# Gated attention's level products and value products, issued as two halves of output rows on the two column halves of TensorE

## The chip, the cores and the metric

The kernel runs on one core of one Trainium2 chip. The metric is the device time of one execution in microseconds. The kernel before was run three times: 564.45, 564.78 and 565.18 us, so its median is 564.78 us. Beside these runs stands one execution under the hardware profiler, from which all rows below are taken.

## What is computed

The reference is one layer of a hybrid decoder over 512 tokens of width 1024: an input projection, three groups of attention heads side by side, an output projection, and a feed-forward block of width 4096, with a norm ahead of each and at the end. The change lies in head group B, a gated linear attention with 4 heads of key width 32 and value width 64:

```python
b = jnp.cumsum(chunks(log_a.reshape(Bsz, S, H, dk)), axis=3)
diff = b[..., :, None, :] - b[..., None, :, :]
decay = jnp.exp(jnp.where(causal[:, :, None], diff, NEG_INF))
attn = jnp.einsum('bhnic,bhnjc,bhnijc->bhnij', qc, kc, decay)
o_intra = jnp.einsum('bhnij,bhnjv->bhniv', attn, vc)
...
o_inter = jnp.einsum('bhnic,bhncv->bhniv', qc * jnp.exp(b), s_prev)
o = (o_intra + o_inter).transpose(0, 2, 3, 1, 4).reshape(Bsz, S, H, dv)
```

A query i sees every earlier key j of its chunk, weighted by a decay for each of the 32 key channels; what lies before the chunk comes through a carried state. The inputs are float32.

## The kernel before, in words

**Order of the work.** The kernel is written as generators ("streams": projections, gated attention, softmax attention, weight splitting, loads, feed-forward) that yield operations. Class Plan (L104 to L206) runs them against a small cost model before anything reaches the chip: each operation has a cost (Op, L40 to L82), each engine a clock, and the operation that can start first is issued next, with ties settled by the streams' priorities. What it issues becomes the fixed order of each engine's instructions. So a changed cost can change the order of later instructions, on all engines. A matmul has a mode, which says whether it uses part of the array's rows (32 or 64 of 128) or of its columns; the model adds SWITCH = 0.2 us where the mode changes (L135 to L138). A list of matmuls is issued as one piece.

**Number formats.** The large products run in float32r with operands split in a high and a low part: for each weight, ScalarE copies the high part (tile wh) and VectorE subtracts it to get the low part (tile wl). The gated attention's products are plain float32; in the profile each such matmul shows as two matmul records with two weight loads.

**The gated attention** (gla, L767 to L881) works with chunks of 128 tokens, four of them (NB). Within a chunk the decay is handled by seven levels (LEVELS = 64, 32, ..., 1; L24): at level L, the token pairs in which the query lies in the second half and the key in the first half of the same block of 2L tokens. For each level, VectorE and ScalarE make a tile kq of scaled keys and queries (levels, L883 to L898). Then TensorE multiplies, for each chunk n and head h, the 32 rows of that head: 128 columns of kq as stationary operand, 64 query columns as moving operand, into a PSUM bank lp[h] (L820 to L828). The four heads lie in four row quarters of the array. Levels go in pairs, 32 matmuls at a time, with 16 for the last level alone. The results are copied to the tiles attn[h], by ScalarE for L >= 32 and by VectorE with a mask else (L829 to L843), and the four banks are freed for others.

Beside it, carry (L900 to L947) makes the carried states. Then the output (L848 to L862, PSUM tiles op): for each chunk, one product of eq (decayed queries, 128 x 128) with the masked state smk[n-1] over all 256 value columns, for n of 1 to 3, and four products of attn[h][:, n, :] (128 x 128, stationary) with the 64 value columns of head h. Two VectorE additions (tiles oB) read the result.

**Around it** TensorE does the value projection (v_proj, tiles vps), the query and key projections (qkps) and, for the softmax attention, scores (sps), transposes (ptp) and values (po, L1023 to L1051). VectorE splits weights (wl), adds up the value projection (v), and computes the softmax's P, mn and rz. The values' products po are already placed on the two column halves: each of a pair of heads writes 64 of the 128 output rows.

## Time and profile before

| what | value |
|---|---|
| three runs, median (lowest to highest) | 564.78 us (564.45 to 565.18) |
| the profiled execution's own time | 566.03 us |
| its span, first to last instruction | 564.0 us |
| TensorE busy, share of the span | 553.6 us, 98% |
| TensorE weight loads | 477.8 us, 85% |
| VectorE busy | 479.6 us, 85% |
| ScalarE busy | 370.3 us, 66% |
| mean granted TensorE clock | 0.997 |

In the profile PE is TensorE's matmul, PEld its weight load, DVE is VectorE, ACT is ScalarE, POOL is GpSimd. A row of the timeline gives start, duration, engine, line, operation, the tiles as out<-in, the form, the count, and in brackets the idle time before it with what ended that. Line L133 is the helper that issues every operation, so rows are told apart by tiles. A matmul's form 32*128 32x64 means 32 rows and 128 columns of the array in use and a moving operand of 32 partitions by 64 elements. The ends of matmuls are modelled, so their pace is read from starts. Of the span, 2.03 us of the execution's own time lie outside it.

### The profile page before, as it was taken

To read this page: it belongs to the slowest core of one execution; us is meant where nothing else is said; L and a number is where in the kernel's file an instruction comes from. 1 tells how busy PE (TensorE), PEld (TensorE's weight loads), DVE (VectorE), ACT (ScalarE), POOL (GpSimd) and SP (SyncE) were. 2 spreads that over 40 slices of the span, in tenths; PEclk is the share of its full clock that TensorE was granted. 3 is DMA by queue.
4 is the path that set the end of the run, shared out by engine and by line. 5 is a ranking of instruction groups with operands and counts; after the bars stand their busy time and mean duration, and the time that the engine had idled before them with its cause. 6 is when DMAs were issued, how large, how long until landed. Compare 5 with 4: busy or idle time off the path is not lost.

```text
span 564.0 us, 9463 instructions
## 1 busy us (share of the span) xinstructions
PE 553.6 (98%) x3513; PEld 477.8 (85%) x3513; DVE 479.6 (85%) x874; ACT 370.3 (66%) x659; POOL 69.0 (12%) x90
## 2 busy tenths in 40 slices
PE   8999999999999999999999999999999999999995
PEld 7977887786876768899987899988999888999884
DVE  5799899978867988999799995799957799867985
ACT  5755744694865775989766476855477655579553
POOL 5003110000010002110111010120020110011103
PEclk9999999999999999999999999999999999999998
DMA  8945594685134765992989429687378594395803
GB/s 301 400 121 118 91 261 95 205 320 112 37 43 121 254 146 112 268 274 60 278 212 209 158 64 279 198 149 206 113 162 279 121 201 160 94 216 113 150 18 131
DMA packets 29948, 96.58 MB, mean 171 GB/s; under 512 B 3648, under 2 KB 3690, under 8 KB 29904
## 3 DMA queue, kind: packets, MB, share of 16 engines
q0 software_dynamic: 9456, 33.53, 33.4%
q1 hardware_dynamic: 20160, 62.20, 30.9%
q8 instruction: 27, 0.44, 0.3%
q10 hardware_dynamic: 288, 0.27, 0.1%
q14 instruction: 17, 0.14, 0.1%
HBM read 93.86 MB, written 2.13 MB: 170 GB/s over the span
## 4 chain that ended last, share of the span: by engine, by line
PE 83%; DVE 9%; DMA 3%; ACT 2%; issue 2%; SPq 0%; DVEq 0%; ACTq 0%; POOLq 0%
PE f2X L133 14%; PE f1X L133 13%; PE qkps L133 10%; PE f1Z L133 8%; PE f2Z L133 7%; PE ops L133 7%; PE vps L133 5%; PE f1Y L133 4%; PE f2Y L133 3%; DMA wraw<-in_w 3%; PE ptp L133 3%; PE po L133 2%; DVE wl L133 2%; PE sps L133 2%; PE av L133 1%
## 5 line engine op out<-in xcount | busy, mean ns | idle before, releaser
L133 DVE TENSOR_TENSOR wl<-wraw,wh 128x1024 fp32r<-128x1024 f32 (+2 forms) x174 | 192.0, 1110 | 39.5 <-ACT wh L133 39.1
L133 ACT ACTIVATE wh<-wraw 128x1024 fp32r<-128x1024 f32 (+2 forms) x173 | 164.6, 966 | 58.1 <-DMA wraw<-in_w 12.3
L133 PE MATMUL f1X<-yp,wh 128*128 128x256 f32 x512 | 92.7, 283 | 0.0
L133 PEld LDWEIGHTS f1X<-yp,wh 128*128 128x128 f32 x512 | 80.1, 192 | 0.3
L133 POOL DMA_DIRECT2D wraw<-in_w x46 | 40.5, 948 | 270.2 <-DVE wl L133 227.2
L133 PE MATMUL f1X<-yp,wl 128*128 128x256 f32 x256 | 72.5, 283 | 0.0
L133 PE MATMUL f2X<-wh,Al 128*128 128x512 f32 (+1 forms) x132 | 50.6, 383 | 0.0
L133 PE MATMUL f2X<-wh,Ah 128*128 128x512 f32 (+1 forms) x132 | 50.6, 383 | 0.0
L133 PE MATMUL f2X<-wl,Ah 128*128 128x512 f32 (+1 forms) x132 | 50.5, 383 | 0.0
L133 PEld LDWEIGHTS f1X<-yp,wl 128*128 128x128 f32 x256 | 49.1, 192 | 0.1
L133 PE MATMUL f1Z<-yp,wh 128*128 128x256 f32 x256 | 46.3, 283 | 0.0
L133 ACT ACTIVATE h<-h 128x512 f32<-128x512 f32 x56 | 34.7, 625 | 10.5 <-DVE h L133 9.9
L133 PE MATMUL qkps<-xh,wh 128*128 128x512 f32 x96 | 40.1, 418 | 0.0
L133 PEld LDWEIGHTS f1Z<-yp,wh 128*128 128x128 f32 x256 | 39.9, 192 | 0.0
L133 ACT ACTIVATE P<-P,mn 128x512 f32<-128x512 f32 (+3 forms) x48 | 26.5, 555 | 18.8 <-DVE mn L133 18.8
L133 ACT ACTIVATE Ah<-h 128x512 fp32r<-128x512 f32 x40 | 24.0, 620 | 21.5 <-DVE h L133 21.5
L133 PE MATMUL qkps<-xh,wl 128*128 128x512 f32 x96 | 37.6, 392 | 0.0
L133 PE MATMUL qkps<-xl,wh 128*128 128x512 f32 x96 | 37.5, 390 | 0.0
L133 PE MATMUL f1Z<-yp,wl 128*128 128x256 f32 x128 | 36.2, 283 | 0.0
L133 DVE TENSOR_TENSOR Al<-h,Ah 128x512 fp32r<-128x512 f32 x40 | 26.9, 686 | 3.2 <-ACT Ah L133 3.1
L133 PEld LDWEIGHTS f2X<-wl,Ah 128*128 128x128 f32 x132 | 24.8, 188 | 4.9
L133 PEld LDWEIGHTS f2X<-wh,Ah 128*128 128x128 f32 x132 | 24.8, 188 | 4.8
(264 smaller groups left out, 1220.8 us busy)
## 6 DMA issues: line engine op xcount, KB each, us to landing
wraw<-in_w SPq DMA_DIRECT2D x66, 512.0 KB, 5.2
wraw<-in_w POOLq DMA_DIRECT2D x46, 512.0 KB, 6.7
wraw<-in_wqk SPq DMA_DIRECT2D x12, 512.0 KB, 6.0
wraw<-in_wv SPq DMA_DIRECT2D x10, 512.0 KB, 6.7
wraw<-in_wv POOLq DMA_DIRECT2D x8, 512.0 KB, 5.4
wraw<-in_wo SPq DMA_DIRECT2D x8, 512.0 KB, 7.1
wraw<-in_wo POOLq DMA_DIRECT2D x8, 512.0 KB, 5.5
nb<-tab SPq DMA_DIRECT2D x12, 256.0 KB, 3.5
```

What stands on the lines that cost most here:

```text
L133: getattr(getattr(self.nc, op.eng), op.method)(*op.args, **op.kw)
```

## The change

The level products are issued in two halves: output rows 0 to 63 for all four heads, then rows 64 to 127, each with half of the stationary columns. The value products likewise, the two halves of a head one after the other; the three products with the carried states now all come ahead of them, and they alone carry the flag that starts an accumulation (start=n < 3: chunks 1 and 2, the first into each of the two banks). Two costs of the model are changed. The amount of arithmetic and the copies out of PSUM stay as they are.

```diff
             elif wide and inner[-1].shape[0] == 32:
-                self.cost = 0.031
+                self.cost = 0.0155
             elif wide:
-                self.cost = 0.002 + max(n / 600 / (1 + (args[0].shape[0] == 64)), 0.21)
+                self.cost = 0.002 + max(n / 600, 0.21) / (1 + (args[0].shape[0] == 64))
...
                 for n in range(NB):
-                    for h in range(4):
-                        c = kq[32 * h:32 * h + 32, n * 128:(n + 1) * 128]
-                        o = lp[h][:, i * 256 + n * 64:i * 256 + (n + 1) * 64]
-                        ops.append(PE.matmul(o.rearrange("p (m l) -> p m l", l=L), c,
-                                             c.rearrange("p (m l) -> p m l", l=2 * L)[:, :, L:], start=True, stop=True))
+                    for rows in (slice(0, 64), slice(64, 128)):
+                        for h in range(4):
+                            c = kq[32 * h:32 * h + 32, n * 128:(n + 1) * 128]
+                            o = lp[h][rows, i * 256 + n * 64:i * 256 + (n + 1) * 64]
+                            ops.append(PE.matmul(o.rearrange("p (m l) -> p m l", l=L), c[:, rows],
+                                                 c.rearrange("p (m l) -> p m l", l=2 * L)[:, :, L:], start=True, stop=True))
...
+        for n in range(1, NB):
+            ops.append(PE.matmul(op_[n // 2][:, n % 2 * 256:n % 2 * 256 + 256], eq[:, n * 128:(n + 1) * 128], smk[n - 1],
+                                 start=n < 3, stop=False, skip_group_check=True))
         for n in range(NB):
-            o = op_[n // 2][:, n % 2 * 256:n % 2 * 256 + 256]
-            vb = vB[n // 2][:, n % 2, :]
-            if n:
-                ops.append(PE.matmul(o, eq[:, n * 128:(n + 1) * 128], smk[n - 1], start=True, stop=False, skip_group_check=True))
-            ops.extend(PE.matmul(o[:, h * 64:(h + 1) * 64], attn[h][:, n, :], vb[:, h * 64:(h + 1) * 64],
-                                 start=(n == 0 and h == 0), stop=h == 3, skip_group_check=True) for h in range(4))
+            for h in range(4):
+                for c in (0, 64):
+                    ops.append(PE.matmul(op_[n // 2][c:c + 64, n % 2 * 256 + h * 64:n % 2 * 256 + (h + 1) * 64],
+                                         attn[h][:, n, c:c + 64], vB[n // 2][:, n % 2, h * 64:(h + 1) * 64],
+                                         start=False, stop=h == 3, skip_group_check=True))
```

## The prediction

> **What bounds the kernel now.** I read the page's totals first, then the chain of waits through the stage that the change touches, then busy times by stage.

> ```profile
> PE 553.6 (98%) x3513; PEld 477.8 (85%) x3513; DVE 479.6 (85%) x874; ACT 370.3 (66%) x659; POOL 69.0 (12%) x90
> ```

> TensorE is busy 98% of the span, so it looks as if any time taken from it shortens the kernel. The chain of waits says where that holds:

> ```profile
> 56.94 1.94 PE lp L133 x64
> 58.88 2.95 PE vps L133 x12
> ...
> 64.43 1.94 PE lp L133 x64
> 66.37 10.42 PE vps L133 x45
> 76.80 1.94 PE lp L133 x64
> 78.74 6.81 PE vps L133 x29
> 85.58 0.67 DVE wl L133
> ...
> 94.83 1.13 DVE wl L133
> ...
> 109.61 0.74 PE ptp L133 x4
> ```

> Three of the four groups of level products (tiles lp) are links of the chain. But at 85.58 us the chain goes over to VectorE and comes back to TensorE only at 109.61. The fourth group (last start at 91.5, by a row below) and the output products (op, from 98.45) lie in that stretch, off the chain. The stages in numbers (us, busy and number of records by engine, granted clock, DMA share and rate):

> ```profile
> 57.00:85.00 28.00, 28.00 (x294) 23.60 (x295) 26.07 (x56) 17.34 (x33) 4.35 (x5) 1.00 0.79 180
> 85.00:104.00 19.00, 19.00 (x133) 15.81 (x133) 19.00 (x44) 10.16 (x18) 0.00 (x0) 1.00 0.37 95
> 104.00:110.00 6.00, 5.51 (x32) 3.83 (x29) 6.00 (x25) 3.93 (x13) 0.00 (x0) 1.00 0.69 198
> 125.00:175.00 50.00, 50.00 (x294) 36.36 (x295) 37.82 (x103) 31.75 (x77) 3.50 (x4) 1.00 0.40 85
> ```

> From 85 to 110 us the third busy column, VectorE, is full: 19.00 of 19.00 and 6.00 of 6.00. TensorE is full too up to 104, and from 104 to 110 it has 0.49 us of idle time. Two engines run abreast, and the later one sets the date at which the stage ends. After that TensorE alone is full (50.00 of 50.00, VectorE 37.82) and carries any lead or delay on to the end. That TensorE already waits for VectorE at the end of the stretch is told by two rows of its timeline:

> ```profile
> 106.91 0.83 PE L133 MATMUL sps<-k,q 64*128 64x256 f32 x6 [0.22 <-DVE mn L133]
> 109.61 0.74 PE L133 MATMUL ptp<-cst,P 128*128 128x128 f32 x4 [0.27 <-DVE P L133]
> ```

> Scores wait for a bank that the softmax's first step reads (mn), transposes for its last (P). A TensorE that gets there sooner waits longer.

> **The change, part by part. Level products.** Under the tile lp the trace counts:

> ```profile
> L133 PE MATMUL lp<-kq x224: 267/270/321, 56.9 to 91.5; 32*128 32x64 f32 x112
> ```

> These 224 records become 448. Four heads run side by side on four row quarters, so 224 are 56 rounds. By the chain's row a group of 64 takes 1.94 us, 0.121 a round or 0.030 a record. What fills a round? Weight loads of op and po (ns, shortest, median and longest), and the list op in the timeline:

> ```profile
> L133 PEld LDWEIGHTS op<-vB,attn x32: 187/192/192, 98.2 to 103.1; 128*128 128x128 f32 x32
> ```

> ```profile
> L133 PEld LDWEIGHTS po<-th,v x96: 132/137/137, 125.9 to 208.1; 128*64 128x64 f32 x96
> ```

> ```profile
> 98.45 1.00 PE L133 MATMUL op<-vB,attn 128*128 128x64 f32 x8
> 99.28 0.65 PE L133 MATMUL op<-m,eq 128*128 128x256 f32 x2
> 99.77 1.00 PE L133 MATMUL op<-vB,attn 128*128 128x64 f32 x8
> ...
> 103.35 1.07 PE L133 MATMUL sps<-k,q 64*128 64x384 f32 x12
> ```

> A weight load of 64 columns lasts 137 ns against 192 for 128 columns: 64 columns cost 55 ns, 128 cost 110. Streaming: the two 256-column records take 99.77 - 99.28 = 0.49 us, 245 ns each, so 64 columns take 61 at most. The eight 64-column records of op ahead of them take 99.28 - 98.45 = 0.83, 104 each, which is a weight load and not the stream. So the level products' 121 ns are a load of 128 columns too, and halves would need 61. That two column halves work at the same time is seen in po:

> ```profile
> 198.86 2.30 PE po L133 x16
> ```

> Its 16 records stream 2 x 2 x (512 + 384 + 256 + 128) = 5120 columns; at 0.96 ns a column one after another that is 4.9 us, and it took 2.30. If eight tiles run abreast, 56 rounds save 121 - 61 = 60 ns each, 3.4 us. Rounds of four may hold other costs (op's pace is 104, not 121), so I take 104 - 55 = 49 ns, 2.7 us in all: 0.8 for each whole group, 0.4 for the fourth. Ends: 3.4 us saved, or worse than nothing if starts have a pace of their own (a rival below).

> **Output products.** 32 records at 104 ns become 32 pairs at 61: 3.33 - 1.95 = 1.4 us saved. The move of the three state products (tiles eq) to the front changes nothing in their number; the price is one more change of the array's tiling, from whole to halves, since the scores that follow have a tiling of their own already. Its price stands around the first group of level products:

> ```profile
> 56.55 0.39 PE L133 MATMUL vps<-wl,xh 128*128 128x512 f32 x1
> 56.87 2.01 PE L133 MATMUL lp<-kq 32*128 32x64 f32 x64
> 58.81 0.50 PE L133 MATMUL vps<-wh,xh 128*128 128x512 f32 x1
> 59.15 0.40 PE L133 MATMUL vps<-wh,xl 128*128 128x512 f32 x1
> ```

> From 56.55 to 56.87 pass 0.32 us and from 58.81 to 59.15 0.34, where such records otherwise follow each other by 0.23 (6.81 us for 29 in the chain): 0.1 us each way, 0.2 together. So the output products save 1.2 us, and 1.4 if the change of tiling hides. The third state product now stands ahead of all value products, so it needs its masked state sooner, by the 24 value records at 104 ns that stood before it (2.5 us), and all value products queue behind it on TensorE. That state is made by VectorE; a wait for it falls into time that is free, as follows.

> **What reaches the end.** TensorE has 2.7 + 1.2 = 3.9 us less to do before 106.91, but the scores there wait for VectorE. VectorE's own work is unchanged: the same copies of the same tiles (attn<-lp), the same additions. It can only end sooner by idle time that goes. Between 57 and 85 it has 28.00 - 26.07 = 1.93 us of that, and after 85 none. The gaps, and what ScalarE (ACT) was doing:

> ```profile
> 61.41 0.43 DVE L133 TENSOR_TENSOR kq<-kB,e 128x256 f32<-128x256 f32 x1 [0.38 <-ACT e L133]
> 64.08 0.43 DVE L133 TENSOR_TENSOR kq<-kB,e 128x256 f32<-128x256 f32 x1 [1.23 <-ACT e L133]
> 81.23 1.23 DVE L133 TENSOR_TENSOR wl<-wraw,wh 128x1024 fp32r<-128x1024 f32 x1 [0.29 <-ACT wh L133]
> ```

> ```profile
> 58.96 1.90 ACT L133 ACTIVATE attn<-lp 64x256 f32<-64x256 f32 x7 [0.27 <-PE lp L133]
> 80.13 1.06 ACT L133 ACTIVATE wh<-wraw 128x1024 fp32r<-128x1024 f32 x1 [2.96 <-PE vps L133]
> ```

> ```profile
> 60.00:64.00 4.00, 4.00 (x25) 3.46 (x24) 2.46 (x7) 3.84 (x12) 0.33 (x1) 1.00 0.73 123
> ```

> The first two gaps wait for the exponentials (e) on ScalarE, which between 60 and 64 is itself busy 3.84 of 4.00 us, mostly with copies of lp. It starts those at 58.96 after 0.27 us of waiting for TensorE; with the group done 0.8 us sooner that wait goes, and all that follows moves up by 0.27 at most. The third gap, 0.29, ends on a weight copy that waited 2.96 us for TensorE; by then TensorE is 2.4 us ahead (three groups), so it goes. Together 0.56 us, and with pauses too short for a bracket some 0.6. Bounds: 0, and all 1.93. I take 0.6, the sum of the waits that have TensorE behind them. After 110 us TensorE carries these 0.6 us to the end. One place can eat them, a wait between 264 and 300 us (us in total, times, longest):

> ```profile
> PEld f2Z L133 <- issue: 0.8, 1, 0.8
> ```

> If its cause does not move up, nothing is left; so 0 stays an end. The profiled execution took 566.03 us (span 564.0 and 2.03 around it), 1.25 above the median of the three runs. On its own time the forecast is 565.4, on the median 564.2.

> **The model's costs.** A level group costs the planner the same as before (64 x 0.0155 = 32 x 0.031), so the order up to op should stay. The list op goes from 3 x 0.429 + 16 x 0.212 = 4.68 to 3 x 0.429 + 32 x 0.107 + 0.2 = 4.91, and po's two shortest products in each pair of heads fall from 0.212 to 0.109, 0.21 a pair, 1.2 over six. From op on, other items can thus win a place. The price by rows: a weight split (wl, 1.13 in the chain) that comes ahead of the softmax or behind it, or 0.2 for a pair of tiling changes; either sign.

> **The rivals.** *Slower: starts have a pace of their own.* Now a record starts every 30 ns on average. If that is not four loads in one round but what starts cost, whatever tile they go to, 448 records take 13.6 us instead of 6.8, the output products 64 x 0.03 = 1.9 instead of 3.3, and TensorE is late by 6.8 - 1.4 + 0.2 = 5.6; the 0.49 us of waits vanish, and the time is 564.8 + 5.1 = 569.9. It decides from 15 ns a start upwards, where halves no longer shorten a group. For it: no row shows a closer mean pace. Against it: op's single tile and lp's four have nearly the same round, 104 and 121 ns, which a price for each start does not explain. [...]

> *Halves take turns.* If two halves of one row quarter load one after the other, a round of eight is two of 55 and more, and nothing is gained: 564.8. Against it stands po, though with 128 rows, not 32.

> *The lead is kept.* If VectorE is not what ends the stage, because the new order takes a weight split out of its way, up to 3.9 us arrive: 560.9; with one split of 1.13 out of the way 0.6 + 1.1, 563.1. Against it: 25.00 of 25.00 us of VectorE.

> *A worse order.* Two weight splits ahead of the softmax, 2.3 us, less 0.6: 566.5. One of them, 565.3, is no measurable loss.

> **How the numbers follow.** A measurement of this kernel can tell about 0.2%, 1.1 us, from no change. Forecast (VectorE keeps the date, 0.6 us gained): 0.52, with its own range from 562.85 (all of 1.93) to 564.8; 0.12 of that is beyond 1.1 us. Halves take turns: 0.10. The lead is kept, wholly or in part: 0.14. A worse order: 0.16, 0.09 of it measurable. Starts' own pace: 0.08. So faster 0.12 + 0.14 = 0.26, slower 0.09 + 0.08 = 0.17, same 0.57. The range leaves out the starts' pace and the far end of the kept lead: it goes from 562.0 (two splits out of the way, 0.6 + 2.2) to 566.8 (the worse order and 0.3, about half of the 0.73 between the shown runs).

> **What would show it.** Right: groups lp of 128 records in 1.1 to 1.3 us, op's group done in some 3.7 instead of 4.9, VectorE still full from 85 to 109, and the idle time of TensorE near 107 to 110 grown from 0.5 to nearly 4 us (3.9 less 0.6 more). Wrong: lp groups of 1.9 us or more (no concurrency, or the pace of starts), VectorE with idle time before 109 (then the lead should have been kept), or an order of wl and P that differs there.

## The result, and the profile after

The changed kernel took 571.31 us (median of five runs, 565.28 to 572.10) beside 565.18 for the kernel before (five runs, 564.45 to 565.94). The ratio on record is 1.0074 with an interval of 1.0049 to 1.0099 (that of the two medians alone is 1.011): slower by 0.7 to 1.1%, where 564.2 us and "no measurable change" were forecast. The changed kernel's five runs also lie further apart, 6.8 us against 1.5; a cause has to explain that too. Three runs of later kernels lie over 1.5% above the fastest of their kernel and are left out of the ratios: 572.16 us in experiment 2, and 680.04 and 1611.22 us in experiments 9 and 10, where nothing on record tells the cause.

The profiled execution of the changed kernel took 568.78 us, span 566.8. The totals hardly differ from before:

```profile
PE 553.2 (98%) x3769; PEld 476.7 (84%) x3769; DVE 479.2 (85%) x870; ACT 372.0 (66%) x663; POOL 69.0 (12%) x90
```

The chain of waits through the stage (start, us, engine, tile, count):

```profile
56.31 1.52 PE lp L133 x91
...
63.40 1.52 PE lp L133 x89
64.93 10.43 PE vps L133 x45
75.36 1.66 PE lp L133 x79
77.02 2.97 issue
79.99 0.36 PE lp L133 x7
80.36 9.11 PE vps L133 x39
```

A group of level products now takes 1.52 us instead of 1.94 (the chain's counts leave out some of the 128 records). The third group stops for 2.97 us, and the chain names no releaser: "issue" means that nothing which the profile shows was waited for. TensorE's timeline there, and at the output products:

```profile
75.29 1.73 PE L133 MATMUL lp<-kq 32*64 32x64 f32 x116
79.99 0.36 PE L133 MATMUL lp<-kq 32*64 32x64 f32 x12 [2.97 <-issue]
...
99.27 1.05 PE L133 MATMUL op<-m,eq 128*128 128x256 f32 x4
100.49 0.70 PE L133 MATMUL op<-s2m,eq 128*128 128x256 f32 x2 [0.17 <-DVE s2m L133]
101.12 2.09 PE L133 MATMUL op<-vB,attn 128*64 128x64 f32 x64
103.14 1.08 PE L133 MATMUL sps<-k,q 64*128 64x384 f32 x12
...
108.15 0.82 PE L133 MATMUL sps<-k,q 64*128 64x256 f32 x6 [1.68 <-DVE mn L133]
109.45 0.66 PE L133 MATMUL ptp<-cst,P 128*128 128x128 f32 x2 [0.47 <-DVE P L133]
```

The stop comes after 116 of 128 records of one list, whose products have their operands already. The output products take 103.14 - 99.27 = 3.87 us instead of 4.90. The two waits for VectorE have grown from 0.22 and 0.27 to 1.68 and 0.47.

The same stretches as before, and then two cut at the places where the granted clock changes (us, busy and records of PE, PEld, DVE, ACT, POOL, granted clock, DMA share, GB/s):

```profile
57.00:85.00 28.00, 25.03 (x431) 20.61 (x415) 23.76 (x50) 15.94 (x31) 4.10 (x5) 1.00 0.77 183
85.00:104.00 19.00, 18.83 (x205) 14.81 (x203) 19.00 (x45) 9.49 (x16) 0.25 (x1) 1.00 0.35 85
104.00:110.00 6.00, 3.84 (x22) 2.86 (x21) 6.00 (x20) 3.94 (x11) 0.00 (x0) 0.92 0.74 206
...
105.64:109.05 3.41, 1.65 (x10) 0.96 (x8) 3.41 (x13) 1.60 (x4) 0.00 (x0) 1.00 0.78 175
109.05:112.47 3.42, 3.02 (x8) 2.14 (x8) 2.70 (x13) 2.90 (x12) 0.00 (x0) 0.50 0.95 371
```

VectorE is full from 85 to 110 as before, but up to 85 it idles 28.00 - 23.76 = 4.24 us instead of 1.93: the stop has reached it. And TensorE runs at half clock from 109.05 to 112.47, behind a stretch of the same length in which it was busy for 1.65 of 3.41 us only; that costs up to 3.42 x 0.5 = 1.7 us. The kernel before has no such stretch: its granted clock is 1.00 from 4.44 to 560.81 us.

Where 2.75 us (568.78 - 566.03) came from, by rows of both timelines. The first group starts 0.63 sooner (56.31, and 56.94 by the chain of before), before any edit has acted. The third starts 1.44 sooner (75.36, 76.80), the value projection behind it 1.62 later (80.36, 78.74): a swing of 3.06, the stop. The scores that wait for VectorE start 1.24 later (108.15, 106.91). Far behind the stage a feed-forward product waits for its weight, in the kernel before and after:

```profile
299.73 0.47 PE L133 MATMUL f2Z<-wh,Ah 128*128 128x512 f32 x1 [0.43 <-ACT wh L133]
```

```profile
302.87 0.47 PE L133 MATMUL f2Z<-wh,Ah 128*128 128x512 f32 x1 [0.41 <-ACT wh L133]
```

It is 3.14 late: 1.9 more since the scores, of which the half clock accounts for up to 1.7.

### The profile page after: what moved, and what is told of

Same layout as the page of the kernel before. It is cut to its first block, busy times and chain, and to the rows that moved or that the text cites. A ratio compares the mean times of both kernels' runs of the same rounds, so it can differ in the third digit from the quotient of the medians.

```text
span 566.8 us, 9972 instructions
## 1 busy us (share of the span) xinstructions
PE 553.2 (98%) x3769; PEld 476.7 (84%) x3769; DVE 479.2 (85%) x870; ACT 372.0 (66%) x663; POOL 69.0 (12%) x90
## 4 chain that ended last, share of the span: by engine, by line
PE 86%; DVE 8%; issue 2%; ACT 2%; DMA 2%; ACTq 0%; POOLq 0%; DVEq 0%
PE f2X L133 14%; PE f1X L133 13%; PE qkps L133 10%; PE f1Z L133 8%; PE f2Z L133 7%; PE ops L133 7%; PE vps L133 6%; PE f1Y L133 4%; PE f2Y L133 3%; PE ptp L133 3%; PE po L133 2%; PE sps L133 2%; DVE wl L133 2%; PE av L133 2%; DMA wraw<-in_w 2%
## 5 line engine op out<-in xcount | busy, mean ns | idle before, releaser
L133 DVE TENSOR_TENSOR wl<-wraw,wh 128x1024 fp32r<-128x1024 f32 (+2 forms) x174 | 191.8, 1109 | 38.9 <-ACT wh L133 36.9
L133 ACT ACTIVATE wh<-wraw 128x1024 fp32r<-128x1024 f32 (+2 forms) x173 | 164.3, 966 | 59.0 <-DMA wraw<-in_w 10.0
L133 PE MATMUL f1X<-yp,wh 128*128 128x256 f32 x512 | 92.7, 283 | 0.0
L133 PEld LDWEIGHTS f1X<-yp,wh 128*128 128x128 f32 x512 | 80.1, 192 | 0.3
L133 POOL DMA_DIRECT2D wraw<-in_w x46 | 40.5, 948 | 270.0 <-DVE wl L133 227.1
L133 PE MATMUL f1X<-yp,wl 128*128 128x256 f32 x256 | 72.5, 283 | 0.0
L133 PE MATMUL f2X<-wh,Al 128*128 128x512 f32 (+1 forms) x132 | 50.5, 383 | 0.0
L133 PE MATMUL f2X<-wh,Ah 128*128 128x512 f32 (+1 forms) x132 | 50.5, 383 | 0.0
L133 PE MATMUL f2X<-wl,Ah 128*128 128x512 f32 (+1 forms) x132 | 50.5, 383 | 0.0
L133 PEld LDWEIGHTS f1X<-yp,wl 128*128 128x128 f32 x256 | 49.1, 192 | 0.0
L133 PE MATMUL f1Z<-yp,wh 128*128 128x256 f32 x256 | 46.3, 283 | 0.0
L133 ACT ACTIVATE h<-h 128x512 f32<-128x512 f32 x56 | 34.7, 625 | 10.5 <-DVE h L133 9.9
L133 PE MATMUL qkps<-xh,wh 128*128 128x512 f32 x96 | 40.2, 419 | 0.0
L133 PEld LDWEIGHTS f1Z<-yp,wh 128*128 128x128 f32 x256 | 39.9, 192 | 0.0
L133 ACT ACTIVATE P<-P,mn 128x512 f32<-128x512 f32 (+3 forms) x48 | 26.5, 552 | 19.4 <-DVE mn L133 19.4
L133 ACT ACTIVATE Ah<-h 128x512 fp32r<-128x512 f32 x40 | 24.1, 620 | 21.5 <-DVE h L133 21.5
L133 PE MATMUL qkps<-xh,wl 128*128 128x512 f32 x96 | 37.6, 392 | 0.0
L133 PE MATMUL qkps<-xl,wh 128*128 128x512 f32 x96 | 37.5, 390 | 0.0
L133 PE MATMUL f1Z<-yp,wl 128*128 128x256 f32 x128 | 36.2, 283 | 0.0
L133 DVE TENSOR_TENSOR Al<-h,Ah 128x512 fp32r<-128x512 f32 x40 | 26.8, 685 | 3.2 <-ACT Ah L133 3.0
L133 PEld LDWEIGHTS f2X<-wl,Ah 128*128 128x128 f32 x132 | 24.8, 188 | 4.9
L133 PEld LDWEIGHTS f2X<-wh,Ah 128*128 128x128 f32 x132 | 24.8, 188 | 4.8
```

Source lines behind the costliest of these rows:

```text
L133: getattr(getattr(self.nc, op.eng), op.method)(*op.args, **op.kw)
```

## The experiments

**Theory.** TensorE runs out of instructions. Beside the data queues the page's third part counts queues for instructions, whose packets take a share of the same 16 engines; the one that grows with the change, before and after:

```profile
q8 instruction: 27, 0.44, 0.3%
```

```profile
q8 instruction: 29, 0.48, 0.3%
```

That is 0.48 MB / 29 = 16.5 KB to a packet; TensorE has 2 x 3769 records, some 260 instructions to a packet. From before to after its records grow by 2 x 256 = 512 and the packets by two, so I take 256 instructions, a block, as my estimate of a packet. The stop behind record 116 of the third group is then the end of a block, some 234 instructions into the list (a weight load and a product to a record, and two waits); from this zero point the other block ends follow by counting, in this program and in every other. Experiment 12 checks that zero point. By the same count a block also ends in the first group (at 56.95 us) and one in the second (at 63.71), and neither stops: an end in a dense list alone is not what stops TensorE, and I take it that the next block is there. A group in halves uses up 256 instructions in 1.5 us; the value projection ahead of it takes 10.43 us for 45 records, 90 instructions. The next packet is seen late, between 77.5 and 79 us (queue: packets, MB, share of the 16 engines); in the nine microseconds before, there is none, and the data queues hold 49.5 + 41.6 = 91% of the engines:

```profile
core 0 of [0], span 566.8 us
q0 software_dynamic: 217, 0.82, 49.5%
q1 hardware_dynamic: 432, 1.57, 41.6%
```

```profile
core 0 of [0], span 566.8 us
q0 software_dynamic: 53, 0.16, 54.0%
q1 hardware_dynamic: 58, 0.24, 43.0%
q8 instruction: 1, 0.02, 4.1%
```

(The first answer is for 68 to 77.5 us, the second for 77.5 to 79; the trace has the packet at 77.77, and the next product starts at 79.99, 2.22 us later.)

**Rival.** The changed costs of the planner gave a worse order of instructions (from just ahead of the output products on, the orders do differ), and the stop is a symptom or chance.

The first four kernels ran on one chip, where the kernel before took 565.44 us (35 runs). Where an experiment needs an order that its costs would not give, costs and modes are set on single operations, and the general costs are those of the kernel whose order is kept, so that the order comes out as named.

**1. The level products alone in halves, order of before.**

```diff
                 for n in range(NB):
-                    for h in range(4):
+                    for rows in (slice(0, 64), slice(64, 128)):
+                        for h in range(4):
...
+            for k, x in enumerate(ops):
+                x.cost, x.mode = 0.031 * (k // 4 % 2), (True, False)
```

> Only the level products are halved; the planner is given the costs and modes of before, so every engine keeps before's order of instructions. Theory A (TensorE runs out of instructions): a group is now 256 TensorE instructions in 1.5 us, and the next block of instructions comes late while the DMA engines are full; the third group again stops for about 3 us near record 116 with no wait shown, and the time is 566 to 572 with a wide spread between runs. Theory B (the changed order of instructions after the output products is the loss): no loss, 564 to 565.5, spread under 1 us.

Median 564.75, ratio 1.0017 (0.9987 to 1.0047), and this hides two clusters: seven runs from 563.34 to 565.43, five from 568.24 to 570.83. The profiled execution, 569.51, is of the second:

```profile
75.90 1.72 PE L133 MATMUL lp<-kq 32*64 32x64 f32 x116
80.86 0.51 PE L133 MATMUL lp<-kq 32*64 32x64 f32 x12 [3.24 <-issue]
```

The stop is there with the old order, behind the same record. The upper five runs have a mean granted clock of 0.991 to 0.993, the lower seven 0.996 to 0.998; so whether the block is late seems to vary from run to run, though only one of these runs has a profile.

**2. Both lists in halves, order of before.**

```diff
+            for k, x in enumerate(ops):
+                x.cost, x.mode = 0.031 * (k // 4 % 2), (True, False)
...
+        state, half = 0.002 + 256 / 600, 0.002 + 0.21
+        for k, x in enumerate(ops):
+            x.mode = False, False
+            x.cost = (state, 0.0, 0.0)[k] if k < 3 else half / 2 + (state / 8 if k >= 19 else 0.0)
```

> Both products halved as in the change, but in before's order of instructions. Theory A: like the change, 567 to 572, with the stop of about 3 us in the third group. Theory B: 563.5 to 565.5, because the order is before's.

Median 567.73 (563.66 to 572.16), ratio 1.002 (0.9993 to 1.0046). Its profiled execution (571.90) stops in the third group for 4.60 us. The runs spread as those of the changed kernel do, though the order is the old one.

**3. Whole products, order of the changed kernel.**

```diff
-                    for rows in (slice(0, 64), slice(64, 128)):
-                        for h in range(4):
+                    for h in range(4):
...
+            for k, x in enumerate(ops):
+                x.cost, x.mode = 0.0155 * (1 if k % 4 else 5), (True, True)
```

> The products of before (whole), in the changed kernel's order of instructions. Theory A: no stop in any group, 564.5 to 566 (the order alone costs or gains under 1 us). Theory B: the loss of the change, about 570.

565.15 (564.46 to 566.05), ratio 0.9992 (0.9982 to 1.0001), no stop in its profile. The order is worth nothing; the rival falls.

**4. The changed kernel, with the block ends moved by 104 instructions.** The warm-up's nine products become 35 small ones, at the same total cost for the planner; nothing else changes.

```diff
-        for _ in range(WARM):
-            yield PE.matmul(warm[:, :128], ones, ones, start=True, stop=True)
+        for _ in range(35):
+            x = PE.matmul(warm[:32, :32], ones[:, :32], ones[:, :32], start=True, stop=True)
+            x.cost, x.mode = WARM * (0.002 + 128 / 600) / 35, (False, False)
+            yield x
```

> The changed kernel with its order, and 26 more warm-up products ahead of everything (35 small ones of 32x32 in place of 9 of 128x128), so that all later TensorE instructions come 104 places later and the block of 256 that began near record 116 of the third group begins near record 65, its forerunner 126 instructions ahead of the group instead of 22. Theory A: the stop in the third group goes or shrinks under 1 us, and the time falls to 564 to 566 with a small spread. Theory B: nothing changes, about 570.

564.56 (563.04 to 566.31), ratio 0.998 (0.9966 to 0.9993). The third group runs through:

```profile
75.80 1.81 PE L133 MATMUL lp<-kq 32*64 32x64 f32 x128
```

More instructions, and 6.8 us below the changed kernel's median. The runs still spread by 3.3 us, more than expected; eight of the twelve have a mean granted clock of 0.994 or 0.995, and the reason follows in experiments 5 and 8. A block still ends in this group, by the count at record 65; but the fifth instruction packet, which in the changed kernel came at 77.77 us, stands in this trace at 65.96. So the shift did not take the ends out of the list: the packet comes ten microseconds ahead of the group (75.80), at a place where the queues had room (in the changed kernel's profile the transfer engines are 0.23 busy from 64 to 68 us, 0.91 from 68 to 77.5). The kernel before with the moved warm-up alone was not run. The next four ran on a chip where the kernel before took 565.50 (35 runs).

**5. The value products alone in halves, order of before** (the second part of the change to the products, with costs as in 2).

> The kernel before with the value products alone in halves, its order of instructions kept. The list of output products has 64 records instead of 32 for its values; the level products stay whole, 128 instructions of TensorE to a group. If TensorE stops because it runs through 256 instructions in 1.5 us before the next block of them has come: no stop here, since this list alone is short of that pace (64 records in 2.1 us) and the transfers are light at 100 us; op done in 3.9 us instead of 4.9, and the time that of the kernel before, 565.0 to 565.4, because VectorE sets the end of the stage. If halves as such bring the loss (any list in halves): 566 or more, with a stop in op or behind it.

565.25, ratio 0.9995 (0.9986 to 1.0005); no stop in its profile. The 64 value records take 2.02 us (98.76 to 100.78) where 3.33 had been counted for 32 whole ones, and the time gains nothing. The profiled run shows more than the expected wait for VectorE:

```profile
103.72:107.13 3.41, 1.63 (x10) 1.03 (x9) 3.41 (x12) 1.98 (x9) 0.00 (x0) 1.00 0.47 99
107.13:110.54 3.41, 3.41 (x12) 2.40 (x12) 3.30 (x18) 2.08 (x9) 0.00 (x0) 0.50 0.99 368
```

Again a stretch in which TensorE idles more than half, and then one at half clock. This was the second cause, not in my theory when the first four ran.

**6. The changed kernel with its third group whole.**

```diff
-                    for rows in (slice(0, 64), slice(64, 128)):
+                    for rows in ((slice(0, 64), slice(64, 128)) if l0 != 4 else (slice(0, 128),)):
```

> The kernel after, with the third group of level products alone whole again (32 matmuls instead of 64); the order of all engines is that of the kernel after, warm-up untouched. If the third group stops for want of instructions: it has 128 of them instead of 256, no block of instructions ends in it, the next one ends 106 instructions behind it, some 10 us later, and nothing stops: 564.5 to 565.2 us, the third group 2.0 us and the other groups 1.5. If the shift of the stop came from the smaller warm-up products of the earlier run and not from where the blocks end, or if dense halves stop wherever they stand: 568 or more, and a stop of about 3 us in the second or the fourth group or behind the third.

565.12 (563.35 to 567.98), ratio 0.999 (0.9976 to 1.0005). No stop in the profiled run (564.47), with the warm-up untouched: 6.2 us below the changed kernel by giving up the halves of one group. The run at 567.98 has a clock of 0.992 and no profile.

**7. The changed kernel with less to transfer at 70 us.** Three weight loads are cut to 64 of 1024 columns, and the split copies read these over and over, so what is computed from them is not the reference's.

```diff
-            yield SP.dma_start(raw[:, :n], src)
+            m = 64 if key in SHORT else n
+            x = SP.dma_start(raw[:, :m], src[:, :m])
+            x.size = 4 * n * 128
+            yield x
...
```

The planner still counts the full size (x.size), so the order stays.

> The kernel after, with three transfers of query and key weights (512 KB each, issued from 69.7 to 75.5 us) cut to 32 KB; the split copies then read these 64 columns sixteen times over, so the arithmetic on them is not the reference's, and no instruction is added or moved. If the block of instructions comes late because the transfer engines are full from 70 to 76 us: it comes by 72 us, the third group runs through in 1.5 to 1.8 us, and the time is 564.0 to 565.0. If the block's delay has nothing to do with the transfers (a fixed time, or it is asked for only when the last one runs out): the stop of about 3 us stays and the time is 568 to 571.

The answer for 68 to 77.5 us now holds the packet which the changed kernel lacks there:

```profile
core 0 of [0], span 565.2 us
q0 software_dynamic: 198, 0.75, 52.9%
q1 hardware_dynamic: 432, 0.59, 17.0%
q8 instruction: 1, 0.02, 0.6%
```

The third group of the profiled run has 128 records in one piece, 1.84 us. So the block was late behind the weights: the data queues now hold 52.9 + 17.0 = 70% of the engines instead of 91%. But the expected 564 to 565 holds only for part of the runs: 565.89 median, ratio 1.0022 (0.9997 to 1.0046), eight runs from 563.54 to 567.19 and four from 569.08 to 570.34. The profiled run itself took 567.19: it has no stop, but a stretch at half clock from 107.84 to 111.25 us. The upper four have no profile; full queues still stand on both sides of the gap that I made (share of the transfer engines 0.91 from 70.30 to 73.71 us, 0.45 up to 77.12, 0.99 up to 80.54), so the stop may remain there. Half confirmed.

**8. Both lists in halves, order of before, block ends moved** (edits of 2 and 4).

> Both lists in halves with the order of the kernel before, and the warm-up in 35 small products instead of 9, which moves all later instructions of TensorE by 104. If the want of instructions is the whole loss: no stop, and 563.4 to 564.2, as the undisturbed runs of that order without the shift had it (563.7 to 563.9), 0.2 to 0.3% faster than the kernel before. If the shift only happened to help the other order: a stop of 3 us in another group, 567 or more in most runs.

564.12 (563.01 to 565.66), ratio 0.9972 (0.996 to 0.9984), as expected; the upper cluster of experiment 2 (566 to 572) is gone. What spread is left goes with the clock: eight runs have a mean granted clock of 0.997 or 0.998 and lie from 563.01 to 564.58, four have 0.994 or 0.995 and lie from 564.21 to 565.66. In its profiled execution (563.44) the wait is long, but no half clock follows:

```profile
105.37 0.83 PE L133 MATMUL sps<-k,q 64*128 64x256 f32 x6 [2.00 <-DVE mn L133]
```

In the stopped execution of experiment 1 both causes are seen together, in stretches of 3.41 us cut where its clock changes:

```profile
76.39:79.80 3.41, 1.23 (x110) 1.09 (x99) 2.25 (x5) 0.00 (x0) 0.86 (x1) 1.00 0.99 248
79.80:83.21 3.41, 2.35 (x17) 1.85 (x17) 1.82 (x5) 0.00 (x0) 0.00 (x0) 0.50 1.06 202
83.21:86.62 3.41, 3.41 (x10) 2.64 (x9) 1.93 (x4) 2.58 (x3) 0.17 (x1) 0.50 0.69 138
86.62:90.00 3.38, 3.38 (x16) 2.81 (x15) 2.71 (x7) 1.83 (x3) 0.69 (x1) 1.00 0.58 88
```

Two stretches at half clock follow the stop, up to 3.4 us more. In the profiled execution of the changed kernel a stop of nearly the same length fell across the border of two stretches:

```profile
74.92:78.33 3.41, 2.10 (x118) 1.54 (x118) 2.98 (x7) 0.81 (x1) 0.14 (x1) 1.00 0.97 167
78.33:81.74 3.41, 1.75 (x18) 1.43 (x18) 1.36 (x5) 0.00 (x0) 0.73 (x1) 1.00 0.78 239
81.74:85.16 3.42, 3.42 (x16) 2.81 (x16) 3.01 (x5) 3.00 (x4) 0.78 (x1) 1.00 0.98 223
```

Along these grids, up to 550 us, the windows of all the profiles can be sorted by TensorE's busy time. After 0.00 (experiment 2), 0.83 (experiment 12), 1.23, 1.59 (experiment 7), 1.63 and 1.65 us the next window was at half clock; after 1.73 us (experiment 6) or more at whole clock it never was. One window falls out, experiment 8's with 1.50. A window that was itself at half clock was followed by another where it was busy for 2.35 or 2.63 us (experiments 1 and 2), not where it was busy for 3.02 or more. So, but for that one, windows a little over half idle were enough.

The last four ran on a chip where the kernel before took 565.07 (25 runs).

**9. As 8, with the wait filled.** Twelve score products are issued ahead of the 384-column scores, rewriting the first pair's result; they lie where TensorE would wait for VectorE.

```diff
+                if p == 0 and qbs == (2, 0):
+                    fill = []
+                    for k in range(12):
+                        rows = slice(64 * (k % 2), 64 * (k % 2) + 64)
+                        x = PE.matmul(at[2, k % 2], qh[rows, 256:384], kh[rows, :384], start=True, stop=False, skip_group_check=True)
+                        x.cost = 0.0
+                        fill.append(x)
+                    ops = fill + ops
                 yield ops
```

> Both lists in halves with the moved blocks of instructions and the order of before, as in the run before it, and 12 more score products (the first pair of the 384-column scores, issued six times ahead of its own start, results unchanged) placed where TensorE would otherwise wait 2 us for VectorE. If TensorE's idle time costs more than itself, because a stretch of 3.4 us with some 1.7 us or more of it idle is followed by a stretch at half clock: the wait at 105 us falls from 2.0 to below 1 us, no run shows a stretch at half clock behind it, all runs lie between 563.0 and 564.3 and the median falls from 564.1 to about 563.3. If the scatter of the runs has another cause: the runs spread from 563 to 565.7 as before, or all are later by the fill.

563.50, seven runs from 562.72 to 564.10, every clock 0.996 or more; ratio 0.9973 (0.9962 to 0.9984). With useless work on TensorE the runs at a lower clock are gone, and with them the upper part of the scatter. The wait that was 2.00 us in experiment 8's profile (first row: the first level products):

```profile
56.06 1.60 PE L133 MATMUL lp<-kq 32*64 32x64 f32 x128
...
105.32 0.83 PE L133 MATMUL sps<-k,q 64*128 64x256 f32 x6 [0.96 <-DVE mn L133]
```

It is the best of the versions, 1.6 us below the kernel before on the same chip, though its ratio cannot be told from that of experiment 8.

**10. The value products in halves, with the same fill.**

> The value products alone in halves, blocks of instructions unmoved, and the same 12 filling score products. Without the fill this kernel's profiled run had a wait of 1.8 us for VectorE and behind it 3.4 us at half clock, and gained nothing (565.25). If the half clock eats the gain: no such stretch now, clocks of all runs 0.996 or more, median 564.6 to 565.0. If VectorE alone sets the date whatever the clock does: 565.2 to 565.5 again, as before.

565.12, or 564.88 over ten runs (563.99 to 565.57); ratio 0.9993 (0.9985 to 1.0002). All clocks are 0.996 or more, as the theory had it, where seven of experiment 5's twelve were 0.994 or 0.995; but the ratio is that of experiment 5. For the time it is inconclusive: whatever the half clock costs this kernel is too small to be told here. Within experiment 5 the seven runs lie from 565.17 to 566.69, the five others from 564.68 to 565.18.

**11. The level products alone, block ends moved** (edits of 1 and 4).

> The level products alone in halves, order of before, the warm-up in 35 small products so that the blocks of instructions end elsewhere. The list op stays whole, so TensorE's lead at 105 us is 1 us smaller and the wait for VectorE about 1 us instead of 2. If the two costs of the change are the stop for instructions and the half clock behind long waits, neither occurs: every run between 563.2 and 564.5, median 563.5 to 563.9, where half of the runs without the shift had 568 to 571. If the stop only needs dense lists: a stop of about 3 us in some group and 568 or more in many runs.

564.67 (564.20 to 565.26), ratio 0.9995 (0.9986 to 1.0003). The upper cluster is gone and its profile has no stop and no half clock, but 563.5 to 563.9 is missed by 0.8. Its stage is no worse than that of experiment 9: from the first level product to the waiting scores both take 49.26 us (56.90 to 106.16, 56.06 to 105.32). What differs in its profile is a start that is 0.84 later, and a wait for a weight far behind the stage:

```profile
56.90 1.59 PE L133 MATMUL lp<-kq 32*64 32x64 f32 x128
...
106.16 0.83 PE L133 MATMUL sps<-k,q 64*128 64x256 f32 x6 [0.48 <-DVE mn L133]
...
299.15 0.47 PE L133 MATMUL f2Z<-wh,Ah 128*128 128x512 f32 x1 [0.41 <-ACT wh L133]
```

Experiment 9's profile has none there. This is the place which the prediction named as able to eat the lead. Why it waits in one kernel and not in the other was not tried.

**12. The first group alone in quarters** (32 output rows each), one execution.

```diff
-                    for rows in (slice(0, 64), slice(64, 128)):
+                    for rows in ((slice(0, 32), slice(32, 64), slice(64, 96), slice(96, 128)) if l0 == 0 else (slice(0, 128),)):
```

> Only the first group of level products is cut further, into four quarters of 32 output rows (256 records of TensorE, 512 instructions); the other groups are whole. It measures the pace of a group where nothing waits. If records start no closer than 12 ns, as 128 of them took 1.52 us: 256 records take 3.0 us or more (stops for instructions left out), and quarters are worse than whole products (1.94). If the 1.52 us are weight loads and streams, which shorten with the number of columns: 0.8 to 1.5 us.

```profile
56.27 2.12 PE L133 MATMUL lp<-kq 32*32 32x64 f32 x195
60.98 0.94 PE L133 MATMUL lp<-kq 32*32 32x64 f32 x61 [2.58 <-issue]
```

It took 569.83 us. 195 records take 2.12 us, 10.9 ns each, with half as many columns in each load as in a group of halves; there 128 records take 1.59 us, counted the same way 12.4 each. So the width of the loads is not what holds a group of halves at 1.52.

The second reading was not planned. In this program a block ends, by the zero point taken from the changed kernel, near the 390th of the group's 512 instructions, at record 195, and there it stops, in a group that had not stopped in any other profile. Counted over all of TensorE's instructions in the traces, the stop comes behind number 1473 in the changed kernel and in experiments 1 and 2, and behind number 961 here: 512 apart, two blocks of 256.

All four stops also end alike. A packet of the instruction queue stands at 77.77 us in the changed kernel, 78.48 in experiment 1, 79.95 in experiment 2 and 58.76 here, and the next product starts 2.2 to 2.4 us later. A block of 128 records in quarters passes in an estimated 1.4 us (128 x 10.9 ns), so in a list of this density a block might come late even over idle queues. Here the queues are full up to 58.5 us (in the changed kernel's profile, whose first group starts at 56.24, the transfer engines are 0.91 busy from 56 to 58.5 us and 0.16 from there to 60), and the two are not told apart.

## Why the prediction was wrong

**Level products: the term was mis-sized.** "In all" 2.7 us were to be saved, from loads of 55 ns a round; groups of "1.1 to 1.3 us" were the sign. They took 1.52, so three groups save 1.3 us and the fourth some 0.2. A round of eight lasts 1.52 / 16 = 95 ns, so 26 ns a round were saved where 49 to 60 were forecast. The starts in the traces tell where the rest went. In the kernel before every round of four but the first follows the last by 111 or 112 ns, its records 6 or 7 ns apart. In the changed kernel's first group the third and the fourth round of eight begin 59 and 58 ns after the one before: the forecast's 61, for the first 32 records. From there on starts come mostly 8 or 17 ns apart, 11.4 on average. So loads did shrink as the prediction had it, and something else then holds the pace; it is not the width of the loads (experiment 12), and what it is stays open.

The mean pace of 11 to 12 ns is like the rival's *starts have a pace of their own*, below the 15 at which I said it would decide, but it is no floor for each start. That the rival's 569.9 lies near the result is chance: at its 30 ns a record a group would take 3.8 us, and it took 1.52, 11.9 ns a record. The trace of the kernel before could have told, by the 6 or 7 ns inside its rounds.

**Output products: right.** 3.87 us where "some 3.7" were forecast; 64 records in 103.14 - 101.12 = 2.02 us, 63 ns a pair against 61. The third state product waited 0.17 us for its masked state, into time that was free, as the text said.

**VectorE holds the date: right.** Full from 85 to 110 in both profiles, and the waits ahead of scores and transposes grew. From 0.49 to 2.15 us in the changed kernel instead of "nearly 4", because the level products saved less. Without a stop the gain that gets past VectorE is 50.04 - 49.26 = 0.78 us from the first level product to the waiting scores (before, and experiments 9 and 11), against 0.6 forecast.

**The order: nearly right.** It did change slightly earlier than "from op on", and was worth nothing (0.9992). So *a worse order* did not come about; *halves take turns* and *the lead is kept* are refuted by 1.52 us a group and by VectorE's 25 us.

**The step that failed:** "After 110 us TensorE carries these 0.6 us to the end", and with it every sentence that let TensorE's idle time be free. It rested on two things that were not looked at. First, that an instruction is there when TensorE wants it. The change doubles instructions in a list that runs at 6 ns an instruction; a block end in the third group meets full transfer queues (0.91 busy from 68 to 77.5 us), and the profiled runs of three such kernels lost 3 to 4.6 us there. No rival had that, though the queue's row stood on the page and could have been set against the new rate: 256 instructions in 1.5 us, in a stage whose transfer engines were 79% busy. Second, that a wait on TensorE costs its own length at most. In this kernel a window of 3.41 us that is half idle or more was, but for one, followed by a window at half clock, up to 1.7 us, and a stop that reached into the next window was followed by two. The waits at 107 us that I counted as the harmless end of the saving are such a window. The two together cover the spread: 565.28 for the run with clock 0.997, 568.78 with the 3 us stop and one half window, 571 to 572 at 0.989 to 0.992, by the clocks two or three half windows. Which gaps those unprofiled runs had is argued from their clocks, not shown.

With both causes taken away, in before's order, the change gains 1.6 us, 563.50 against 565.07, where 0.6 was forecast. Of that the profiles show 0.78 us in the stage. Experiment 9's profile also starts its first group 0.81 us sooner (56.06, 56.87 before) and lacks the wait for a weight near 300 us; neither is explained.

What stays open: how the window's activity is counted. Experiment 8's profile has one busy for 1.50 us of 3.42 without a half clock behind it, while 1.63 and 1.65 had one:

```profile
101.87:105.29 3.42, 1.50 (x7) 0.92 (x5) 3.42 (x10) 1.99 (x5) 0.00 (x0) 1.00 0.41 102
105.29:108.70 3.41, 3.02 (x16) 2.04 (x16) 3.41 (x19) 2.72 (x12) 0.00 (x0) 1.00 0.97 233
```

So it is not record time alone; kinds of products may count differently. This was not tried.

## What to carry to other kernels

When a list is cut into smaller instructions, count instructions per microsecond as well as columns, find where the instruction blocks end in it (here 256 to a block, by the estimate above), and look at the transfer queues in the microseconds ahead; if a block ends there while the queues are full, moving it by a few harmless instructions is a cheap test and was here a cheap cure (104 instructions, 571.31 to 564.56 us). Do not book idle time on TensorE at nothing: here one of about half a clock window could cost as much again (1.76 of 3.41 us idle, then 3.42 us at clock 0.50), and since the grid lay elsewhere in each profile (half clock from 109.05, 107.13 and 107.84 us in the changed kernel and experiments 5 and 7), it shows as runs in clusters and must be read from the clocks of all. Where a lead ends in an unavoidable wait, useless products in it can keep the clock, as here (0.996 or more in all seven runs of experiment 9).

## What the runs showed of the hardware

Records on eight or sixteen small tiles of the array came at a mean of one per 11.9 and 10.9 ns, with rounds of eight at 58 and 59 ns among the first 32 records of a group; on one whole tile they had started every 104 ns, on four every 30. Blocks of instructions came late by whole microseconds while weight transfers held the queues (0.91 busy from 68 to 77.5 us in the changed kernel; stops of 2.58, 2.97, 3.24 and 4.60 us), at the end of a block by the count of 256 (an estimate from 512 more instructions in two more packets), in four programs and at two places, and each stop ended 2.2 to 2.4 us after a packet of the instruction queue. A gap of 2.97 us was followed by no half clock in one execution, one of 3.24 us by two windows of it in another, by where they lay on a grid of 3.41 us.
